# Transposing x before its norm, and a head of five column tiles

## The chip, the cores and the metric

The kernel runs on one core of a Trainium2 chip. The metric is device time in microseconds. A core has TensorE (PE in the profile; PEld are its weight loads), VectorE (DVE), ScalarE (ACT), GpSimd (POOL) and SyncE (SP, which here issues nearly all transfers).

## The reference

One layer of a hybrid decoder trunk, in float32, for 1024 prompt positions and 64 sample positions (8 sequences of 8) of 1024 channels. Cut to what matters:

```python
h = rmsnorm(x, g_norm)              # x * rsqrt(mean(x*x) + eps) * g_norm
proj = h @ w_in                     # 1024 x 3200, 25 columns of 128
bg_a, cg_a, v_a, z_a, a_b, g_b, z_b, q_x, z_x = split(proj)
out_a = bg_a * causal_dwconv3(cg_a * v_a) * silu(z_a)
u_b   = a_b * sigmoid(g_b)
out_b = silu(layernorm(causal_dwconv31(u_b))) * silu(z_b)
out_x = cross_attn(q_x, k, v) * silu(z_x)       # k, v from rmsnorm(mem, g_mem)
y = rmsnorm(x + concat(out_a, out_b, out_x) @ w_out, g_final)
```

The new states of both convolutions and the prompt's k and v are returned too.

## The kernel before, in words

Everything is kept transposed: channels on the 128 partitions, the 1088 positions along the columns. A float32 product is made of three fp32r products: each operand is split into a high part (a copy rounded to fp32r, on ACT) and a low part (the rest, on DVE), and high x high, low weight x high and high weight x low are summed in PSUM. `hh[k]` and `hl[k]` are the high and low part of h for row block k of 8; `whi[n]`, `wlo[n]` those of column tile n of `w_in`. All three passes of one column tile over one chunk of positions are 24 matmuls (`proj`), into one of four `MM` banks of PSUM; four `SD` banks serve all else. `CHUNKS` are 256, 384 and 448 positions. `order` lists the 25 column tiles; `evac` takes a finished chunk out of PSUM and does what its kind asks for. When a tile's chunk is done, `w_split` prepares a half of the next tile's weights.

`startup` is issued in the order in which it is written. It loads x0, x1, three columns of weights, then x2 to x8, a fourth column, the memory tokens, the small parameters and a fifth column, all on SP's queue; g_norm and g_mem (8 rows of 128 each, into one tile `graw`) come on ACT's queue. PE runs twelve filler matmuls (`WARM`). x0 and x1 are squared, their norm factors worked out (`rstd_chain`), the rows scaled, transposed on PE, and taken out of PSUM multiplied by g_norm (`x_ev`: the high part on ACT, then the low part on DVE). The first three column tiles are multiplied for chunk 0, then for chunk 1, while the other x tiles are squared, scaled and transposed (`x_tr`, and `x_T` as side steps).

Behind it the loop over n does chunk 2 of tiles 0 to 2 and all chunks of tiles 3 to 24. Side work stands in the list `steps`; `side()` does one step after each fourth matmul. The 31 taps of the long convolution are 1024-column operations on DVE in the list `taps`; after each chunk `run_taps` issues `taps_per(n)` of them (2) at a priority 100 places lower, and at n = 19 the rest. The output projection of nine row tiles ends the kernel.

Every tile of SBUF beside the small ones comes from a pool of 45 slots of 1088 columns. The transfers share eight completion semaphores in turn, so that one waits for the one eight places before.

Of the kernel before, what the change touches and what calls it, by code (L numbers as in the profile page):

```python
# [16 lines left out]
KT = 8  # L17
# [13 lines left out]
WARM = 12  # L31
CHUNKS = [(0, 256), (256, 384), (640, 448)]
# [3 lines left out]
def hybrid_trunk_kernel(  # L36
# [73 lines left out]
    def taps_per(n):  # L110
        return T1 if n < 11 else T2
# [15 lines left out]
    sig0s = cst.tile([128, NS], F32, name="sig0s")  # L127
# [3 lines left out]
    graw = cst.tile([16, 128], F32, name="graw")  # L131
# [34 lines left out]
    def x_load(i):  # L166
        xt[i] = B("x", cols=D)
# [32 lines left out]

    def x_T(c, k):
        x_ev(c, k, x_tr(c, k))

    def x_tr(c, k):
        off, n = CHUNKS[c]
        ps = SD()
        for i in groups[c]:
            o = xcols[i] - off
            tr(ps[:, o:o + 128], xt[i][:, k * 128:(k + 1) * 128], 128)
        return ps  # L210

    def x_ev(c, k, ps):
        off, n = CHUNKS[c]
        S.activation(hh[k][:, off:off + n], ps[:, :n], AF.Copy, scale=gT[:, k:k + 1])
# [8 lines left out]
        [("g", 0, 15), ("a", 0, 12), ("cg", 0, 3), ("v", 0, 6), ("bg", 0, 0)]  # L223
        + [("g", 1, 16), ("a", 1, 13), ("g", 2, 17), ("a", 2, 14)]
# [7 lines left out]
    raw, whi, wlo = {}, {}, {}  # L232

# [94 lines left out]
    def pieces(c):  # L328
        off, n = CHUNKS[c]
        np_ = min(off + n, SEQ) - off  # L330
        return off, n, np_, n - np_

    def ev_g(c, ps, j):
        off, n, _, _ = pieces(c)
        if c == 0:
            sig[j] = B("sig")
        if j == 0:
            S.copy(sig[j][:, off:off + n], ps[:, :n])
        else:
            S.activation(sig[j][:, off:off + n], ps[:, :n], AF.Sigmoid)  # L340

    def ev_a(c, ps, j):
        off, n, p, s = pieces(c)
        if c == 0:
            u_p[j] = B("u")
            G.memset(u_p[j][:, 0:30], 0.0)
        if j == 0:
            S.copy(u_p[j][:, 30 + off:30 + off + p], ps[:, :p])
            if s:
                S.copy(sig0s, ps[:, p:n])  # L350
                glu0()
            return
        V.tensor_tensor(u_p[j][:, 30 + off:30 + off + p], ps[:, :p], sig[j][:, off:off + p], ALU.mult)
        dv(p / 0.96 + 70)
# [9 lines left out]
    def glu0():  # L364
        S.activation(sig[0], sig[0], AF.Sigmoid)
        V.tensor_tensor(u_p[0][:, 30:30 + SEQ], u_p[0][:, 30:30 + SEQ], sig[0][:, :SEQ], ALU.mult)
        V.tensor_tensor(
            u_s[0][:, 240:304].rearrange("p (t b) -> p t b", b=NB), tb(sig0s), tb(sig[0][:, SEQ:NT]), ALU.mult,
        )
        V.tensor_copy(u_s[0][:, 304:334], u_p[0][:, SEQ:SEQ + 30])  # L370
        queue_taps(0)

    def ev_q(c, ps, j):
        off, n, p, s = pieces(c)
        if c == 0:
# [547 lines left out]
    def startup():  # L923
        nc.scalar.dma_start(graw[0:8, :], g_norm[0].rearrange("(k p) -> k p", p=128))
        V.memset(epst, EPS)
        S.activation(warm, epst, AF.Sqrt)
        for i in (0, 1):
            x_load(i)
        for n in range(3):
            w_load(n)  # L930
        nc.scalar.dma_start(graw[8:16, :], g_mem[0].rearrange("(k p) -> k p", p=128))
        for i in range(2, 9):
            x_load(i)
        w_load(3)
        mem_load()
        load_params()
        w_load(4)
        make_identity(nc, ident)
# [3 lines left out]
        wps = SD()  # L942
        for _ in range(WARM):
            T.matmul(wps[:, :128], ident, ident, start=True, stop=True)  # L944
        T.transpose(wps[:, 256:272], graw, ident[:16, :16])
        norm = [Norm([xt[i] for i in g], [xrows[i] for i in g]) for g in ([0], [1], groups[1], groups[2])]
        norm[0].square(0)
        norm[0].chain()
        norm[1].square(0)
        norm[0].factor()  # L950
        norm[1].chain()
        norm[0].scale_act(0)
        norm[1].scale(0)
        V.tensor_copy(gT, wps[:, 256:272])
        w_hi(0, S.copy)
        banks = [SD(), SD(), SD(), MM(), MM(), MM()]
# [7 lines left out]
        w_lo(0)
        w_hi(1, G.tensor_copy)
        pr = [MM()]
        for k in range(KT):
            x_ev(0, k, banks[k])
            pass_k(0, 0, pr[0], 0, k)
            if k in (1, 2):  # L970
                banks.append(SD())
                x0_tr(k + 5, 0)
                x0_tr(k + 5, 1)
            else:
                T.matmul(wps[:, :128], ident, ident, start=True, stop=True)  # L975
        pr += [MM(), MM()]
        w_lo(1)
        w_hi(2, S.copy)
        w_lo(2)
        n1, n2 = norm[2], norm[3]  # L980
        for i in range(3):
            n1.square(i)
        n1.chain()
        n1.scale(0)
        n1.scale(2, G)
        n1.scale(1)
        for n, p in ((0, 1), (1, 0), (0, 2), (1, 1), (1, 2)):
            pass_(n, 0, pr[n], p)
        evac(0, 0, pr[0])
        evac(1, 0, pr[1])  # L990
        for p in range(3):
            pass_(2, 0, pr[2], p)
        n2.square(0)
        n2.square(1)
        evac(2, 0, pr[2])
        t1 = [x_tr(1, k) for k in range(4)]
        pr = [MM(), MM(), MM()]
# [13 lines left out]
        for n in range(3):  # L1011
# [4 lines left out]
        for n in range(3):  # L1016
            pass_(n, 1, pr[n], 2)
            side()
            evac(n, 1, pr[n])
        flush_steps()  # L1020


    if True:
        with tc.manual_schedule():
            startup()
        for n in range(0, NCT):
            if n < 3:
# [82 lines left out]
            for c in range(3) if n > 2 else (2,):  # L1110
# [60 lines left out]
```

## Time and profile before

| | us |
|---|---|
| median of 3 runs | 477.63 (477.08 to 477.91) |
| profiled execution | 478.5 |
| its span | 476.7 |
| PE busy | 465.8 |
| DVE busy | 318.3 |
| ACT busy | 221.8 |
| chunk 2 of tile 0 begins | 41.55 |
| tile 3 begins | 57.2 |

The granted clock over the profiled run is 0.998. In the profile a line number names the line of the kernel that issues the instruction; all matmuls of the products have line 89, all transposes of tiles line 96, and all operations of DVE line 53, since helpers issue them. What an instruction writes and reads stands as `out<-in` by the names of tiles. Busy time of PE holds modelled ends, so prices of matmuls are read from start to start.

### The profile page before, as it was taken

The page shows a single profiled execution, that of the slowest core. Times are in us where ns is not written, and L with a number is a line of the kernel's source. Part 1 is how long each engine was busy: PE and PEld are TensorE (multiplying, and loading weights), DVE is VectorE, ACT ScalarE, POOL GpSimd, SP SyncE. Part 2 cuts the span into 40 slices and gives each one's busy share as a digit, 9 for nine tenths or more (in the row PEclk, how much of TensorE's full clock was granted, in tenths as well). Part 3 has the DMA queues.
Part 4 walks back from the last instruction along what each step waited for, and adds up shares of the span by engine and source line. Part 5 has one row for each costly group of instructions (what it writes and reads, how often), then busy time and mean ns, then how long its engine had stood idle before and what let it go on. Part 6 is the DMA issues. An engine that isn't in the chain of part 4 may idle for free.

```text
span 476.7 us, 7269 instructions
## 1 busy us (share of the span) xinstructions
PE 465.8 (98%) x2850; PEld 427.6 (90%) x2850; DVE 318.3 (67%) x547; ACT 221.8 (47%) x573; POOL 10.3 (2%) x24
## 2 busy tenths in 40 slices
PE   6999999999999999999999999999999999999994
PEld 5999999999999999999999998999999888888884
DVE  3687699966959899889479598633563446333334
ACT  6884480340215359457592545558852533211111
POOL 4110000000000000000000000000000000000000
PEclk9999999999999999999999999999999999999999
DMA  9970321004440400111020521023501653211111
GB/s 281 347 235 15 103 74 45 0 1 107 118 131 5 129 0 1 45 44 46 2 83 6 177 88 32 16 58 97 170 0 46 211 208 119 79 45 45 45 61 71
DMA packets 39166, 40.42 MB, mean 85 GB/s; under 512 B 1647, under 2 KB 34325, under 8 KB 39125
## 3 DMA queue, kind: packets, MB, share of 16 engines
q1 hardware_dynamic: 39101, 39.96, 26.7%
q8 instruction: 22, 0.36, 0.3%
q14 instruction: 11, 0.09, 0.1%
q10 hardware_dynamic: 32, 0.01, 0.0%
HBM read 34.81 MB, written 5.42 MB: 84 GB/s over the span
## 4 chain that ended last, share of the span: by engine, by line
PE 97%; DVE 1%; POOL 1%; issue 0%; ACT 0%; DVEq 0%; POOLq 0%; ACTq 0%
PE mm L89 83%; PE sd L89 6%; PE sd L96 5%; PE sd L944 1%; PE sd L794 1%; DVE wl L53 0%; PE sd L975 0%; POOL x L169 0%; POOL stb L501 0%; DVE yg L53 0%; ACT sd L902 0%; POOL qblk L503 0%; DVEq L1167 0%; DVE xres L53 0%; POOL prow L491 0%
## 5 line engine op out<-in xcount | busy, mean ns | idle before, releaser
L89 PE MATMUL mm<-hh,wh 128*128 128x256 f32 (+2 forms) x600 | 118.9, 333 | 0.0
L89 PE MATMUL mm<-hl,wh 128*128 128x256 f32 (+2 forms) x600 | 117.0, 332 | 0.0
L53 DVE SCALAR_TENSOR_TENSOR accB<-u,prm,accB 128x1024 f32<-128x1024 f32 x90 | 115.4, 1282 | 1.5
L89 PE MATMUL mm<-hh,wl 128*128 128x256 f32 (+2 forms) x600 | 115.0, 330 | 0.0
L89 PEld LDWEIGHTS mm<-hh,wh 128*128 128x128 f32 x600 | 98.3, 189 | 5.0 <-issue 1.3
L89 PEld LDWEIGHTS mm<-hl,wh 128*128 128x128 f32 x600 | 97.7, 189 | 4.6 <-issue 1.3
L89 PEld LDWEIGHTS mm<-hh,wl 128*128 128x128 f32 x600 | 98.2, 189 | 3.9 <-issue 0.3
L89 PE MATMUL mm<-wol,mh 128*128 128x512 f32 (+1 forms) x136 | 51.3, 378 | 0.0
L89 PE MATMUL mm<-woh,mh 128*128 128x512 f32 (+1 forms) x136 | 51.3, 377 | 0.0
L89 PE MATMUL mm<-woh,ml 128*128 128x512 f32 (+1 forms) x136 | 51.2, 377 | 0.0
L53 DVE TENSOR_TENSOR xres<-mm,xres 128x512 f32<-128x512 f32 (+2 forms) x19 | 12.5, 662 | 40.4 <-PE mm L89 40.4
L872 ACT ACTIVATE sd<-xres 128x512 f32<-128x512 f32 (+1 forms) x16 | 9.6, 602 | 58.9 <-DVE xres L53 58.9
L53 DVE TENSOR_TENSOR wl<-wr,wh 128x512 fp32r<-128x512 f32 x50 | 33.6, 698 | 4.0 <-ACT wh L245 2.4
L89 PEld LDWEIGHTS mm<-woh,mh 128*128 128x128 f32 x136 | 25.6, 188 | 5.0 <-ACT woh L245 0.4
L89 PEld LDWEIGHTS mm<-wol,mh 128*128 128x128 f32 x136 | 25.6, 188 | 4.9 <-DVE wol L53 0.3
L89 PEld LDWEIGHTS mm<-woh,ml 128*128 128x128 f32 x136 | 25.6, 188 | 4.7
L245 ACT CAST wh<-wr 128x512 fp32r<-128x512 f32 x44 | 25.9, 623 | 0.0
L297 ACT ACTIVATE prod<-us,prm 128x64 f32<-128x64 f32 x93 | 23.6, 342 | 0.0
L640 ACT ACTIVATE P<-sd,nb 128x256 f32<-128x256 f32 x32 | 14.8, 473 | 16.5 <-DVE nb L53 16.4
L440 ACT ACTIVATE sz<-mm 128x256 f32<-128x256 f32 (+2 forms) x24 | 11.3, 472 | 22.0 <-PE mm L89 22.0
L340 ACT ACTIVATE sig<-mm 128x256 f32<-128x256 f32 (+2 forms) x6 | 2.8, 474 | 33.5 <-PE mm L89 33.5
L380 ACT CAST Q<-mm 64x384 fp32r<-64x384 f32 (+1 forms) x12 | 5.3, 439 | 23.6 <-PE mm L89 23.5
(191 smaller groups left out, 519.1 us busy)
## 6 DMA issues: line engine op xcount, KB each, us to landing
wr<-in_w_in_dram SPq DMA_DIRECT2D x25, 512.0 KB
x<-in_x_prompt_dram SPq DMA_DIRECT2D x8, 512.0 KB
wor<-in_w_out_dram SPq DMA_DIRECT2D x8, 512.0 KB
xres<-in_x_prompt_dram SPq DMA_DIRECT2D x8, 512.0 KB
out_dram<-xres SPq DMA_DIRECT2D x7, 512.0 KB
cache<-in_cache_mem_k_dram SPq DMA_DIRECT2D x8, 256.0 KB
cache<-in_cache_mem_v_dram SPq DMA_DIRECT2D x8, 256.0 KB
mem<-in_mem_prompt_dram SPq DMA_DIRECT2D x2, 512.0 KB
```

Source lines behind the costliest of these rows:

```text
L53: r = f(*a, **k)
L89: T.matmul(out, lhsT, rhs, start=start, stop=stop)
L96: T.transpose(out, in_, ident[:n, :n])
L245: S.copy(dst_hi[:, a:b], src[:, a:b])
L297: S.activation(p3[:, k, :], src, AF.Copy, scale=w[:, k0 + k:k0 + k + 1])
L340: S.activation(sig[j][:, off:off + n], ps[:, :n], AF.Sigmoid)
L380: S.copy(q[a, off:off + p], ps[a, :p])
L440: S.activation(sz[0][:, off:off + n], ps[:, :n], AF.Silu)
L640: S.activation(P_[i][:, h * 256:h * 256 + 256], bank[h // 2][:, (h % 2) * 256:(h % 2) * 256 + 256], AF.Exp, bias=nb[:, h:h + 1], scale=SCA ...
L794: T.transpose(ps[:, j * 128:j * 128 + 128], accB[j][:, lncols[i]:lncols[i] + 128], ident)
L872: S.activation(junk[:rows], xr[:rows, cs], AF.Square, accum_out=ss[:rows, f:f + 1])
L944: T.matmul(wps[:, :128], ident, ident, start=True, stop=True)
```

## The change

It lets the first two x tiles be transposed as they come and puts their norm factor in later.

- The first 256 positions are transposed without their norm; `hh`, `hl` hold g_norm times x there. The two norm factors are spread over a 128 x 128 block each (`fb`), transposed on PE and kept as a row `rrow`, the same on all partitions, and chunk 0 of the first five column tiles is multiplied by it as it leaves PSUM (`take`). Behind the head `rescale(k)` puts the norm into `hh`, `hl` for the other tiles, one step for each k.
- The head has five column tiles (`NHEAD`), and four of them (`NROW`) are loaded by rows: for each k one transfer of 128 rows by 512 columns. For each k the matmuls run over four tiles. `order` begins with the three a tiles, g0 and cg0; so a is stored first and multiplied by the sigmoid of g later, in SBUF.
- x0 and x1 come in halves, woven with the row blocks of weights; x2 to x7 and the fifth column follow. g_mem is loaded on SP's queue behind x7, into the same 8 rows as g_norm, and transposed after row block 6; x8, the memory tokens and the parameters are loaded behind it.
- The chunks of the first five tiles stay 256, 384, 448; the other twenty have 384, 384, 320.
- `WARM` is 5, the fillers among the first matmuls are gone, and the identity is made first. Three taps a chunk are issued in tiles 5 to 8.

In the diff `p(k, j)` is pass j of row block k over the four tiles, `hi` and `lo` are the two halves of `x_ev` for chunk 0, `hw_hi` and `hw_lo` the split of a row block of weights.

```diff
+HEAD = [(0, 256), (256, 384), (640, 448)]
+REST = [(0, 384), (384, 384), (768, 320)]
+NHEAD = 5
+NROW = 4
+RAW = HEAD[0][1]
...
     def taps_per(n):
-        return T1 if n < 11 else T2
+        return 3 if 5 <= n < 9 else T1 if n < 11 else T2
...
+    def rescale(k):
+        a, b = hh[k][:, :RAW], hl[k][:, :RAW]
+        t = B("t", cols=RAW)
+        V.tensor_tensor(t, a.bitcast(F32), b.bitcast(F32), ALU.add)
+        V.tensor_tensor(t, t, rrow[0], ALU.mult)
+        S.copy(a, t)
+        V.tensor_sub(b, t, a.bitcast(F32))
...
+    def hw_load(k):
+        if k % 2 == 0:
+            hrw[k // 2] = B("wr", cols=D)
+        c0 = order[0][2] * 128
+        nc.sync.dma_start(hrw[k // 2][:, hsl(k)], w_in[0, k * 128:(k + 1) * 128, c0:c0 + 512])
...
+    def take(dst, ps, n):
+        if rawc[0]:
+            V.tensor_tensor(dst, ps[:, :n], rrow[0][:, :n], ALU.mult)
+        else:
+            S.copy(dst, ps[:, :n])
...
     def startup():
+        make_identity(nc, ident)
         for i in (0, 1):
+            x_half(i, 0)
+        for k in range(3):
+            hw_load(k)
+        for i in (0, 1):
+            x_half(i, 1)
+        hw_load(3)
+        x_load(2)
+        hw_load(4)
+        hw_load(5)
+        x_load(3)
+        hw_load(6)
+        hw_load(7)
+        x_load(4)
+        w_load(4)
+        for i in range(5, 8):
             x_load(i)
...
+        nc.sync.dma_start(graw, g_mem[0].rearrange("(k p) -> k p", p=128))
...
+        n0.square(0)
+        hw_hi(3, S.copy)
+        banks += [SD() for _ in range(4)]
+        for i in (0, 1):
+            for k in range(4, 8):
+                x0_tr(k, i)
+        for k in range(4, 8):
+            hi(k)
...
+        for k in range(3, KT):
+            if k > 3:
+                hw_hi(k, S.copy)
+                hw_lo(k)
+            p(k, 0)
+            p(k - 1, 1)
+            p(k - 1, 2)
+            if k == 5:
+                n0.square(1)
+                n0.chain()
+                n0.factor()
+                fb = B("fb", cols=RAW)
+                for i in (0, 1):
+                    V.tensor_scalar(
+                        fb[:, i * 128:i * 128 + 128], ident, 0.0, n0.f[:, i:i + 1], ALU.mult, ALU.add
+                    )
+            if k == 6:
+                rps = SD()
+                for i in (0, 1):
+                    tr(rps[:, i * 128:i * 128 + 128], fb[:, i * 128:i * 128 + 128], 128)
+                T.transpose(rps[:, 256:264], graw, ident[:8, :8])
+                n1.square(0)
+                rrow[0] = B("rrow", cols=RAW)
+                S.copy(rrow[0], rps[:, :RAW])
+                S.copy(gT[:, 8:16], rps[:, 256:264])
...
+        n1.square(1)
+        n1.square(2)
         n1.chain()
+        n1.factor()
+        w_hi(4, S.copy)
+        w_lo(4)
         n1.scale(0)
+        n1.scale_act(1)
+        n1.scale(2)
+        pr4 = SD()
+        for n in range(NROW):
+            evac(n, 0, acc[n])
+        for j in range(3):
+            pass_(4, 0, pr4, j)
+        evac(4, 0, pr4)
+        t1 = [x_tr(1, k) for k in range(3)]
...
+                if k + 3 < KT:
+                    t1.append(x_tr(1, k + 3))
+        for i in range(4):
+            n2.square(i)
...
+                    for k in range(KT):
+                        steps += [mk(rescale, k)]
```

More of the change, by code (lines that the diff above doesn't have):

```diff
@@ L204, in x_tr @@
     def x_tr(c, k):
-        off, n = CHUNKS[c]
+        off, n = HEAD[c]
         ps = SD()
@@ L326, in hybrid_trunk_kernel, with chunks, pieces, us_new @@
     ms = [None]
-    def pieces(c):
-        off, n = CHUNKS[c]
+    def chunks(n):
+        return HEAD if n < NHEAD else REST
+    def pieces(ch):
+        off, n = ch
         np_ = min(off + n, SEQ) - off
         return off, n, np_, n - np_
+    rawc, rrow = [False], [None]
+    def take(dst, ps, n):
+        if rawc[0]:
+            V.tensor_tensor(dst, ps[:, :n], rrow[0][:, :n], ALU.mult)
+            dv(n / 0.96 + 70)
+        else:
+            S.copy(dst, ps[:, :n])
+    def us_new(j):
+        return u_s[j][:, 240:304].rearrange("p (t b) -> p t b", b=NB)
@@ L333, in ev_g, with ev_a @@
+    def ev_a(c, ps, j):
+        off, n, p, s = pieces(c)
+        if c[0] == 0:
+            u_p[j] = B("u")
+            G.memset(u_p[j][:, 0:30], 0.0)
+        take(u_p[j][:, 30 + off:30 + off + p], ps, p)
+        if s:
+            S.copy(us_new(j), tb(ps[:, p:n]))
     def ev_g(c, ps, j):
-        off, n, _, _ = pieces(c)
-        if c == 0:
+        off, n, p, s = pieces(c)
+        if c[0] == 0:
             sig[j] = B("sig")
         if j == 0:
-            S.copy(sig[j][:, off:off + n], ps[:, :n])
+            take(sig[j][:, off:off + n], ps, n)
+            if s:
+                S.activation(sig[0], sig[0], AF.Sigmoid)
+                V.tensor_tensor(u_p[0][:, 30:30 + SEQ], u_p[0][:, 30:30 + SEQ], sig[0][:, :SEQ], ALU.mult)
+                dv(1140)
@@ L339, in ev_g @@
         else:
             S.activation(sig[j][:, off:off + n], ps[:, :n], AF.Sigmoid)
[L342 to L354, printed above, removed]
+            u = u_p[j][:, 30 + off:30 + off + p]
@@ L389, in ev_cg @@
         off, n, _, _ = pieces(c)
-        if c == 0:
+        if c[0] == 0:
             cgt[0] = B("cg")
-        S.copy(cgt[0][:, off:off + n], ps[:, :n])
+        take(cgt[0][:, off:off + n], ps, n)
     def ev_v(c, ps, j):
         off, n, p, s = pieces(c)
-        if c == 0:
+        if c[0] == 0:
             s_p[j] = B("s")
@@ L453, in evac @@
         kind, j, _ = order[n]
+        c = chunks(n)[c]
+        rawc[0] = n < NHEAD and c[0] == 0
         if kind == "zA":
@@ L923, in startup @@
     def startup():
-        nc.scalar.dma_start(graw[0:8, :], g_norm[0].rearrange("(k p) -> k p", p=128))
+        nc.scalar.dma_start(graw, g_norm[0].rearrange("(k p) -> k p", p=128))
         V.memset(epst, EPS)
         S.activation(warm, epst, AF.Sqrt)
+        make_identity(nc, ident)
         for i in (0, 1):
-            x_load(i)
[L929 to L938, printed above, removed]
+            x_half(i, 0)
[13 more added lines that the diff above has]
+        for i in range(5, 8):
+            x_load(i)
         for k in range(KT):
@@ L941, in startup @@
             hl[k] = B("hl", F32R)
-        wps = SD()
+        wps = MM()
         for _ in range(WARM):
             T.matmul(wps[:, :128], ident, ident, start=True, stop=True)
[L945 to L956, printed above, removed]
+        T.transpose(wps[:, 256:264], graw, ident[:8, :8])
+        V.tensor_copy(gT[:, 0:8], wps[:, 256:264])
+        xt[8] = B("x", cols=D)
+        norm = [Norm([xt[i] for i in g], [xrows[i] for i in g]) for g in groups]
+        n0, n1, n2 = norm
+        nc.sync.dma_start(graw, g_mem[0].rearrange("(k p) -> k p", p=128))
+        banks = [SD() for _ in range(4)]
         def x0_tr(k, i):
@@ L961, in startup @@
         for i in (0, 1):
-            for k in range(6):
+            for k in range(4):
                 x0_tr(k, i)
[L964 to L982, printed above, removed]
+        acc = [MM() for _ in range(NROW)]
+        def p(k, j):
+            for n in range(NROW):
+                pass_k(n, 0, acc[n], j, k)
+        def hi(k):
+            x_ev_hi(0, k, banks[k])
+        def lo(k):
+            x_ev_lo(0, k, banks[k])
+        hw_hi(0, G.tensor_copy)
+        hi(0)
+        hi(1)
+        hw_hi(1, S.copy)
@@ new lines, in startup @@
+        lo(0)
+        lo(1)
+        hw_lo(0)
+        p(0, 0)
+        hi(2)
+        hi(3)
+        hw_hi(2, S.copy)
+        hw_lo(1)
+        lo(2)
+        p(1, 0)
+        lo(3)
+        p(0, 1)
+        p(0, 2)
+        hw_lo(2)
+        p(2, 0)
+        p(1, 1)
+        p(1, 2)
+        x_load(8)
+        mem_load()
+        load_params()
+        w_load(5)
+        n0.square(0)
[4 more added lines that the diff above has]
+                x0_tr(k, i)
@@ new lines, in startup @@
+        for k in range(4, 8):
+            hi(k)
+        hw_lo(3)
+        for k in range(4, 8):
+            lo(k)
+        for k in range(3, KT):
[23 more added lines that the diff above has]
+                S.copy(gT[:, 8:16], rps[:, 256:264])
@@ L983, in startup @@
+        for n in range(NROW):
+            for j in (1, 2):
+                pass_k(n, 0, acc[n], j, KT - 1)
+        n1.square(1)
+        n1.square(2)
         n1.chain()
+        n1.factor()
+        w_hi(4, S.copy)
+        w_lo(4)
         n1.scale(0)
[L985 to L997, printed above, removed]
+        n1.scale_act(1)
+        n1.scale(2)
+        pr4 = SD()
+        for n in range(NROW):
+            evac(n, 0, acc[n])
[3 more added lines that the diff above has]
+        t1 = [x_tr(1, k) for k in range(3)]
+        pr = [MM() for _ in range(NROW)]
         for k in range(KT):
             x_ev(1, k, t1[k])
-            for n in range(3):
+            for n in range(NROW):
@@ L1010, in startup @@
         n2.scale(3)
-        for n in range(3):
+        for n in range(NROW):
             pass_(n, 1, pr[n], 1)
@@ L1015, in startup @@
             steps.append(mk(x_T, 2, k))
-        for n in range(3):
+        for n in range(NROW):
             pass_(n, 1, pr[n], 2)
-            side()
             evac(n, 1, pr[n])
+        pr4 = MM()
+        for j in range(3):
+            pass_(4, 1, pr4, j)
+        evac(4, 1, pr4)
         flush_steps()
@@ L1109, in hybrid_trunk_kernel @@
                 wo_load(worder[2])
-            for c in range(3) if n > 2 else (2,):
+            for c in range(3) if n >= NHEAD else (2,):
                 proj(n, c)
```

77 lines of the change are left out of this document (45 added, 32 removed).

## The prediction

> **What bounds the kernel now.** I read the shares of busy time and the chain of work that ended last first, then stretches of the start, then the timeline of the start engine by engine. Shares by engine, and the chain's shares:
>
> ```profile
> PE 465.8 (98%) x2850; PEld 427.6 (90%) x2850; DVE 318.3 (67%) x547; ACT 221.8 (47%) x573; POOL 10.3 (2%) x24
> PE 97%; DVE 1%; POOL 1%; issue 0%; ACT 0%; DVEq 0%; POOLq 0%; ACTq 0%
> ```
>
> TensorE is the chain. So the time is TensorE's work, plus what it loses before the stream of matmuls is closed, plus a tail the change does not touch. Stretches (busy us of PE, PEld, DVE, ACT, POOL with counts; then clock, DMA share, GB/s):
>
> ```profile
> 0.00:5.00 5.00, 0.66 (x3) 0.66 (x4) 0.06 (x1) 2.44 (x3) 3.50 (x14) 1.00 0.63 220
> 5.00:10.00 5.00, 5.00 (x25) 4.74 (x24) 2.55 (x12) 4.00 (x9) 0.11 (x1) 1.00 1.16 303
> 11.00:18.00 7.00, 6.93 (x58) 6.46 (x57) 6.60 (x14) 6.81 (x15) 0.52 (x1) 1.00 1.03 410
> 18.00:21.00 3.00, 3.00 (x28) 3.00 (x27) 2.30 (x7) 2.05 (x6) 1.31 (x1) 1.00 1.15 190
> 57.20:118.00 60.80, 60.80 (x353) 56.86 (x353) 52.44 (x68) 22.45 (x61) 0.25 (x2) 1.00 0.15 44
> ```
>
> From 5 us on PE counts as busy, but the 25 instructions of 5 to 10 us are mostly the warm-up filler (line 944). The timeline of the start (start, duration, engine, instruction, count):
>
> ```profile
> 4.05 1.06 ACT L182 ACTIVATE junk<-x 128x1024 f32<-128x1024 f32 x1 [1.20 <-DMA x<-in_x_prompt_dram]
> 4.34 5.49 PE L944 MATMUL sd<-ident 128*128 128x128 f32 x24 [4.34 <-POOL ss L177]
> 9.89 1.63 POOL L253 CAST wh<-wr 128x512 fp32r<-128x512 f32 x2 [5.56 <-DMA wr<-in_w_in_dram]
> 10.88 0.49 PE L96 MATMUL sd<-ident,x 128*128 128x128 f32 x3
> 11.19 1.21 ACT L214 ACTIVATE hh<-sd,gT 128x256 fp32r<-128x256 f32 x3 [1.98 <-PE sd L96]
> 11.21 0.49 PE L96 MATMUL mm<-ident,x 128*128 128x128 f32 x3
> 11.99 1.26 DVE L53 SCALAR_TENSOR_TENSOR hl<-sd,gT,hh 128x256 fp32r<-128x256 f32 x3
> 14.06 1.19 ACT L253 CAST wh<-wr 128x512 fp32r<-128x512 f32 x2
> 15.12 2.48 DVE L53 TENSOR_TENSOR wl<-wr,wh 128x512 fp32r<-128x512 f32 x4
> 16.14 1.10 ACT L182 ACTIVATE junk<-x 128x1024 f32<-128x1024 f32 x1
> 17.18 1.10 ACT L182 ACTIVATE junk<-x 128x1024 f32<-128x1024 f32 x1
> 18.40 0.30 ACT L141 ACTIVATE y<-ss,epst 128x3 f32<-128x3 f32 x1
> 19.54 1.54 DVE L53 TENSOR_SCALAR x<-x,y,t 128x1024 f32<-128x1024 f32 x2
> 41.55 1.87 PE L89 MATMUL mm<-hh,wh 128*128 128x448 f32 x8
> ```
>
> Prices from it, start to start: a transpose 0.11 us (three from 10.88 to 11.21), an x high part 0.40 on ACT, its low part 0.42 on DVE, a weight half 0.60 on ACT and 0.62 on DVE, a square 1.04, square root to first scaling 1.1, a scaling 0.77. Matmuls by width, from a closed stretch of one column tile, and two out-projection matmuls nine apart:
>
> ```profile
> 155.90 1.12 PE L89 MATMUL mm<-hh,wl 128*128 128x256 f32 x8
> 156.86 1.12 PE L89 MATMUL mm<-hl,wh 128*128 128x256 f32 x8
> 159.22 1.55 PE L89 MATMUL mm<-hh,wl 128*128 128x384 f32 x8
> 160.60 1.55 PE L89 MATMUL mm<-hl,wh 128*128 128x384 f32 x8
> 163.64 1.81 PE L89 MATMUL mm<-hh,wl 128*128 128x448 f32 x8
> 165.29 1.81 PE L89 MATMUL mm<-hl,wh 128*128 128x448 f32 x8
> ...
> 400.00 0.39 PE L89 MATMUL mm<-woh,ml 128*128 128x512 f32 x1
> ...
> 402.04 0.39 PE L89 MATMUL mm<-woh,ml 128*128 128x512 f32 x1
> ```
>
> Eight from start to start: 0.96/8 = 120 ns at 256 columns, 1.38/8 = 173 at 384, 1.65/8 = 206 at 448; and 2.04/9 = 227 at 512.
>
> **What the start loses now.** The first matmul of the third chunk starts at 41.55 us. Useful work before it: 72 transposes x 0.109 = 7.85, 72 matmuls x 0.12 = 8.64, 72 x 0.1735 = 12.49; sum 28.98. Lost: 12.6 us. This is the account in which the new head must do better; it waits today for x, its squares and root, its scaling, and then a column of weights.
>
> **The new start, step by step.** Norm off the path: the transposes need only the first halves of x0 and x1 (2 x 262 KB) and the first weight block (262 KB), 0.79 MB together. The first stretch moved 1.1 MB by 5.0 us, so 0.79 MB has moved by about 4.1; x0 in the row of 4.05 us came 0.6 us after its bytes by that rate; the first block is there at 4.7, its POOL cast (half of 1.63) ends at 5.6. The identity is now made ahead of POOL's memsets, so PE warms from about 1.6 us; at the slow 0.23 us of line 944, ten filler instructions and eight transposes end near 5.7, the first high part near 6.1. Start of useful matmuls 6.1 against 11.7 now.
>
> From there to the transpose of g_mem (after row block k = 6) PE has 19 groups of four matmuls x 0.48 = 9.1, eight transposes 0.9, two of the norm row 0.2: 10.2. ACT has 8 x 0.40 + 6 x 0.60 + 2 x 1.04 + 0.2 = 9.1, but twice stands in PE's way (the square of x0 ahead of the fourth weight block; four x parts ahead of the fifth): PE waits about 1.3. Arrival at the transpose: 6.1 + 10.2 + 1.3 = 17.6 us; work done by then 16 transposes 1.7 + 9.1 + 0.2 = 11.0, lost 6.6.
>
> **The wait that the change adds.** The g_mem load moves from ACT's queue to SP's, behind x0 to x7, eight weight blocks and one column of weights: 4.19 + 2.10 + 0.52 = 6.82 MB. What a place in that queue means, from SP's timeline and its waits:
>
> ```profile
> 11.63 0.39 SPq L239 DMA_DIRECT2D wr<-in_w_in_dram  x1
> ...
> 23.39 0.22 SPq L497 DMA_DIRECT2D prow<-in_ln_g_dram  x1
> ...
> SPq L497 <- DMA wr<-in_w_in_dram: 1.3, 1, 1.3
> ```
>
> A weight column issued at 11.63 landed at 23.4, when line 497, which waited for it, went: transfers land in turn, 11.8 us after issue here. So: 1.10 MB by 5.0 us, 5.20 MB in 2 to 4 KB pieces at 410 GB/s 12.7 us, 0.52 MB in 512-byte pieces at 303 GB/s 1.7, landing 0.6: g_mem at 20.0 us. PE waits 2.4. Behind that transpose stand PE's row block 7 and, on ACT, the copies of the norm row and of g_mem and the high part of weight block 7: another 1.3 us (0.2 + 0.2 + 0.6 and handovers). Then x3's and x4's squares stand ahead of the fifth tile's weights on ACT: 2.1 + 0.2 + 0.6 against 2.4 us of PE work, and its low parts wait for the norm chain on DVE: PE waits 1.1. Scaling of x4 and the four evacuations (0.42 each, now on DVE with the multiplication by the norm row) cost 0.4 before chunk 1. Last, all four squares of the third x group now stand behind chunk 1's high parts:
>
> ```profile
> 27.98 1.05 ACT L182 ACTIVATE junk<-x 128x1024 f32<-128x1024 f32 x1
> ...
> 31.46 2.33 POOL L197 TENSOR_SCALAR x<-x,y,t 128x1024 f32<-128x1024 f32 x1 [9.41 <-ACT y L141]
> ```
>
> Now two squares start at 27.98 and the scalings end at 34.4, 6.4 us later; two more squares make it 8.5, against 1.3 + 32 x 0.1735 + 0.7 = 7.6 of PE work, with handovers in PE's favour: I take 0.4. Lost by the third chunk: 6.6 + 2.4 + 1.3 + 1.1 + 0.4 + 0.4 = 12.2. The start gains only **0.4 us**: what the norm's removal gives, g_mem takes back. Bounds: without the wait at g_mem about 2.4 better; with 1.5 us more waiting, 1.1 worse.
>
> The Trainium skill, "DMA: Bandwidth & Descriptors", section "Where 436 GB/s comes from", says that for HBM to SBUF the HBM side binds at about 358 GB/s for a core. The trace does not agree: 410 over 7 us. By the page 5.20 MB would take 14.5 us, g_mem would land at 21.8 and the time come out 1.8 us higher (an estimate from the page's figure).
>
> **Chunks 384, 384, 320 for 20 column tiles.** Each has 24 steps of one matmul per chunk: 480 steps. Before, 120 + 173.4 + 206.5 = 499.9 ns. 320 columns is not in the trace. Its neighbours 256 and 384 put it at 146.7; but 448 stands 6.3 ns over the middle of its neighbours 384 and 512, and 320 is such an odd multiple of 64 too: 153.0. So 493.5 to 499.8 ns: a gain of 0.0 to 3.1 us; neither is nearer, I take the middle, **1.5 us**.
>
> The skill's "TensorE: Matmul & The Clock Gate", Part 1, gives a warm matmul as its columns over 2.4 GHz plus a fixed 2.5 ns. The rows show 13 ns fixed, and 20 at 448. By the page's form a split of 1088 columns in three would always cost the same, and this gain be nil.
>
> **Edits I cost at nothing, and their cover.** The rescaling of 256 columns is 8 x (three DVE operations and one ACT copy):
>
> ```profile
> L53 DVE TENSOR_TENSOR tA<-mm,tA 128x256 f32<-128x256 f32 x3 | 1.3, 420 | 0.0
> L53 DVE SCALAR_TENSOR_TENSOR accB<-u,prm,accB 128x1024 f32<-128x1024 f32 x90 | 115.4, 1282 | 1.5
> 92.79 1.29 DVE L53 TENSOR_TENSOR wl<-wr,wh 128x512 fp32r<-128x512 f32 x2
> ...
> 104.24 1.12 PE L89 MATMUL mm<-hh,wl 128*128 128x256 f32 x8
> ```
>
> 8 x 3 x 0.42 = 10.1 us of DVE, under five third chunks of 24 x 0.2065 = 4.96 us, 24.8 in all, before tile 5 reads them; uncovered it would be 10.1. Tile 5's two weight halves (1.2) and the parameter copies share it, with 13.5 left for those, so the cover holds. Fewer filler matmuls: they are not counted as useful on either side. x8 and the two memory tiles now follow g_mem on SP, 1.31 MB or 3.2 us at 410 GB/s: there by 24, and first squared near 35; late, each us would add one. The g_mem issue itself also waits until PE has read g_norm from the same tile, near 4 us, long before its turn. Taps: tiles 5 to 8 take three a chunk, 12 more than now, 12 x 1.28 = 15.4 us of DVE, where the like stretch (57.2 to 118.0) leaves 8.4 idle. So DVE falls some 7 us behind there. What PE needs of DVE there is made early: the low half weights of 92.79 are used at 104.24. Taps also stand 100 places lower in priority. I take 0, up to 3.1 as below.
>
> **Sum.** 0.4 + 1.5 = 1.9 us less. The profiled execution took 478.5 us (span 476.7), 0.9 over the median of the runs, 477.63; 478.5 - 1.9 = 476.6, and against the median 475.7. Differences under 0.2% (0.95 us) can't be told from none in this kernel.
>
> **Rivals.**
> 1. g_mem does not hold PE up (a small transfer might pass). Then 2.4 us less: 473.3. Against it: it needs 5.7 MB in the 12 us after 5.0, over 470 GB/s, or a way past the queue, where line 497's row shows none. 0.14.
> 2. 320 columns cost 153 ns, the split of columns is worth nothing: 475.7 + 1.5 = 477.2. For it the odd 448 row. 0.15.
> 3. Slower: DVE in tiles 5 to 8. If a tile's low weights queue behind the overload (7.0) and that chunk's taps (3.9), 10.9 us, they come after the lead that they have, two chunks and a pass, 24 x (173.4 + 150) ns + 1.4 = 9.2, less 0.6 + 0.7 for the split itself: PE waits about 3.1, once, since waiting refills the lead: 478.8. It decides where the backlog passes some 4 us ahead of the weights. 0.20.
> 4. Transfers run for part of the way as in the stretch of 18 to 21 us (190 GB/s): half a megabyte so takes 2.7 us for 1.3, g_mem comes 1.5 us later, 477.2. 0.10. The skill's 358 GB/s, on the page named above, would come out on this side too.
>
> **Numbers.** My forecast 0.41 (475.7; by itself 473.9 to 477.2), the rivals as given. Faster by over 0.2% (below 476.7): 0.36 of mine, 0.14, 0.02 of the others: 0.52. Within: 0.28; slower 0.20. The range reaches from rival 1 with the full 3.1 of the chunks, 473.3 - 1.6 = 471.7, rounded in to 472.2, to rival 3 with no gain from chunks, cut to 479.6.
>
> **What would show it.** Right: PE's first real matmul near 6 us; a PE wait of 2 to 3 us near 17 to 20 that ends with the g_mem load; the third chunk starting with 12.2 us lost; matmuls of 384, 384, 320 adding to about 497 ns; no PE wait on DVE from tile 5 to 8. Wrong: no wait at g_mem (rival 1), a 320 row at 153 (2), low weights or evacuations ending PE waits in tiles 5 to 9 (3), or a clock under 1.00 after 10 us.

## The result: slower, 482.96 us, and the profile after

The changed kernel takes 482.96 us (median of 4, 482.16 to 483.20) against 477.77 us for the kernel before on the same chip: a ratio of 1.011, interval 1.0094 to 1.0126. That is 5.2 us slower, where 1.9 us faster was forecast, and it lies above the forecast range. The profiled execution took 482.8 us, its span 481.0, 4.3 more than before.

The page's shares by engine and of the chain, after the change:

```profile
PE 464.2 (97%) x2827; PEld 432.8 (90%) x2827; DVE 324.4 (67%) x573; ACT 225.8 (47%) x586; POOL 7.1 (1%) x22
PE 65%; DVE 22%; ACT 5%; DMA 4%; issue 3%; SPq 0%; DVEq 0%; ACTq 0%
```

PE's busy share hardly moved, 98 to 97%. The chain tells more: TensorE held 97% of it, and now 65%, with 22% on VectorE. VectorE's share of the whole span is still 67%, so a mean over the span could not have warned of this; the stretches below do. Two places matter, and the first is the start. PE's timeline after the change (start, duration, instruction, count; in brackets the idle time before it and what ended that):

```profile
7.05 1.40 PE L96 MATMUL mm<-hh,wh 128*128 128x256 f32 x8 [1.06 <-POOL wh L276]
...
17.97 0.38 PE L103 MATMUL sd<-ident,fb 128*128 128x128 f32 x2
22.91 0.23 PE L1094 MATMUL sd<-ident,graw 8*128 8x8 f32 x1 [4.56 <-DMA graw<-in_g_mem_dram]
24.18 1.22 PE L96 MATMUL mm<-hh,wh 128*128 128x256 f32 x4 [1.05 <-ACT wh L276]
25.20 1.05 PE L96 MATMUL mm<-hh,wl 128*128 128x256 f32 x4
26.06 1.05 PE L96 MATMUL mm<-hl,wh 128*128 128x256 f32 x4
...
59.91 1.40 PE L96 MATMUL mm<-hh,wh 128*128 128x448 f32 x6
```

PE comes to the transpose of g_mem near 18.2 us and stands until 22.91, when the load lands. Behind it come 1.05 us for the last weight block's high part on ACT. Then the matmuls themselves are slow: four of 256 columns take 0.86 us from 25.20 to 26.06, 215 ns each instead of 120. The last row is the first matmul of the third chunk. Stretches of the same execution (PE, PEld, DVE, ACT, POOL busy with counts; clock, DMA share, GB/s):

```profile
0.00:5.00 5.00, 3.61 (x16) 3.27 (x17) 0.23 (x2) 1.49 (x2) 0.83 (x9) 1.00 0.54 161
5.00:10.00 5.00, 3.94 (x28) 3.42 (x28) 3.60 (x7) 3.81 (x9) 3.29 (x6) 1.00 1.03 361
10.00:15.00 5.00, 4.59 (x40) 4.39 (x39) 3.59 (x7) 4.02 (x9) 0.00 (x0) 1.00 1.04 406
15.00:20.00 5.00, 3.35 (x29) 3.11 (x27) 2.08 (x9) 1.94 (x5) 0.13 (x1) 1.00 1.09 366
20.00:22.90 2.90, 0.00 (x0) 0.00 (x0) 0.00 (x0) 0.00 (x0) 0.00 (x0) 1.00 1.04 332
25.00:30.00 5.00, 5.00 (x25) 5.00 (x25) 3.46 (x10) 3.69 (x8) 0.16 (x2) 0.51 0.45 156
63.00:84.00 21.00, 21.00 (x109) 19.30 (x108) 3.23 (x14) 4.71 (x9) 0.10 (x1) 1.00 0.28 88
85.00:225.00 140.00, 138.32 (x871) 133.85 (x869) 138.36 (x184) 67.57 (x200) 0.10 (x1) 1.00 0.20 57
```

The granted clock is 0.51 between 25 and 30 us; by the trace's clock record it fell to half at 23.0 us, 4.7 us after PE began to stand, and came back at 29.9. So the idle stretch cost its own length and then half of TensorE's speed. The Trainium skill, "TensorE: Matmul & The Clock Gate", Part 1, says that an idle window of about 3.4 us sets the array back to half clock; this trace agrees (4.56 us idle, then 0.51), but in e10, below, shorter waits also did it.

The last row is the second place: VectorE is busy for 138.36 of 140 us. The same stretch before the change:

```profile
85.00:225.00 140.00, 140.00 (x895) 132.62 (x894) 118.55 (x152) 62.09 (x185) 0.22 (x2) 1.00 0.19 53
```

20 us more work on VectorE in that stretch, and 1.7 us less of PE busy. Where the work came from: the taps of the long convolution alone (the instructions on `accB`) by stretches, before the change:

```profile
40.00:63.00 23.00, 0.00 (x0) 0.00 (x0) 5.77 (x5) 0.00 (x0) 1.00 0.27 79
63.00:85.00 22.00, 0.00 (x0) 0.00 (x0) 8.30 (x8) 0.00 (x0) 1.00 0.12 38
85.00:225.00 140.00, 0.00 (x0) 0.00 (x0) 71.26 (x59) 0.00 (x0) 1.00 0.19 53
```

The same view after the change, where nothing stands ahead of 85 us, and the first tap of its timeline:

```profile
85.00:225.00 140.00, 0.00 (x0) 0.00 (x0) 82.25 (x68) 0.00 (x0) 1.00 0.20 57
```

```profile
85.14 0.81 DVE L60 TENSOR_SCALAR accB<-u,prm 128x1024 f32<-128x1024 f32 x1
```

The new order runs the three a tiles, then g0. The taps of `u` need a times the sigmoid of g0 for all positions, and g0 is the fourth of five tiles in the third chunk. Before the change 14.1 us of taps were done by 85 us, and now none. VectorE works 3.2 us of the 21 from 63 to 84, and is full from then on. Of the 20 us, 11 are taps (82.25 - 71.26); the rest is other work that came earlier before, the memory tokens' operands and the short convolution's sums among it.

How that reaches TensorE, around one weight column after the change: ACT, DVE, PE.

```profile
178.27 1.27 DVE L60 SCALAR_TENSOR_TENSOR accB<-u,prm,accB 128x1024 f32<-128x1024 f32 x1
179.47 0.16 DVE L60 TENSOR_SCALAR nb<-mx 128x4 f32<-128x4 f32 x1
...
179.70 1.28 ACT L701 ACT_TABLE_LOAD   x1 [8.21 <-DVE nb L60]
...
183.18 0.65 ACT L299 CAST wh<-wr 128x512 fp32r<-128x512 f32 x1
...
183.87 0.96 PE L96 MATMUL mm<-hh,wh 128*128 128x384 f32 x4 [0.57 <-ACT wh L299]
...
193.58 0.66 PE L96 MATMUL sd<-PT,kv 128*64 128x128 f32 x8 [0.66 <-ACT PT L721]
```

The negated maxima `nb` of the attention scores come behind taps on VectorE. ACT's exponentials wait for them, 8.21 us at this place, and the next weight cast (`wh`) stands behind the exponentials in ACT's order, so PE waits for ACT. The chain of PE's waits alone would name ACT; ACT's own wait names the maxima. Over the stretch 180 to 220 us three waits of PE, start to start less the price of the matmul, make 2.2 us (0.73, 0.83, 0.61).

Checkpoints of the two profiled executions, before and after: tile 11 of the order begins at 166.9 and 170.3 us (+3.4); tiles 11 to 14 take 64.0 and 65.8 (+1.9); from tile 15 to the first matmul of the output projection 144.3 and 143.6 (-0.7); the rest -0.3. The sum is the 4.3 of the spans.

### The profile page after: what moved, and what is told of

It is laid out like the page before. It is cut to its first block, busy times and chain, and to the rows that moved or that the text cites. A ratio compares the mean times of both kernels' runs of the same rounds, so it can differ in the third digit from the quotient of the medians.

```text
span 481.0 us, 7290 instructions
## 1 busy us (share of the span) xinstructions
PE 464.2 (97%) x2827; PEld 432.8 (90%) x2827; DVE 324.4 (67%) x573; ACT 225.8 (47%) x586; POOL 7.1 (1%) x22
## 4 chain that ended last, share of the span: by engine, by line
PE 65%; DVE 22%; ACT 5%; DMA 4%; issue 3%; SPq 0%; DVEq 0%; ACTq 0%
PE mm L96 56%; DVE accB L60 11%; PE sd L103 4%; PE sd L96 4%; DMA graw<-in_g_mem_dram 2%; DVE tA L60 2%; DVE wl L60 2%; DMA x<-in_x_prompt_dram 1%; DVE Q L60 1%; DVE red L60 1%; DVE mx L60 1%; DMA wr<-in_w_in_dram 1%; ACT sd L870 1%; ACT junk L188 1%; DVE wml L60 1%
## 5 line engine op out<-in xcount | busy, mean ns | idle before, releaser
L96 PE MATMUL mm<-hh,wh 128*128 128x384 f32 (+3 forms) x592 | 117.0, 334 | 3.1 <-ACT wh L276 1.5
L96 PE MATMUL mm<-hl,wh 128*128 128x384 f32 (+3 forms) x592 | 117.6, 333 | 0.0
L96 PE MATMUL mm<-hh,wl 128*128 128x384 f32 (+3 forms) x592 | 114.9, 331 | 0.0
L96 PEld LDWEIGHTS mm<-hl,wh 128*128 128x128 f32 x592 | 99.4, 190 | 2.0 <-issue 1.3
L96 PEld LDWEIGHTS mm<-hh,wl 128*128 128x128 f32 x592 | 99.9, 190 | 1.3 <-issue 0.3
L299 ACT CAST wh<-wr 128x512 fp32r<-128x512 f32 x40 | 23.3, 625 | 0.1
L499 ACT ACTIVATE sz<-mm 128x384 f32<-128x384 f32 (+1 forms) x24 | 11.3, 472 | 20.3 <-PE mm L96 20.2
L238 ACT ACTIVATE hh<-sd,gT 128x256 fp32r<-128x256 f32 (+2 forms) x24 | 12.8, 563 | 12.5 <-PE sd L103 12.2
L422 ACT ACTIVATE sig<-mm 128x384 f32<-128x384 f32 (+1 forms) x6 | 2.8, 472 | 31.3 <-PE mm L96 31.3
```

The costliest lines, as they stand in the source:

```text
L96: T.matmul(out, lhsT, rhs, start=start, stop=stop)
L299: S.copy(dst_hi[:, a:b], src[:, a:b])
L499: S.activation(sz[0][:, off:off + n], ps[:, :n], AF.Silu)
```

## Experiments

Two theories. **Head:** PE's wait for g_mem, with the half clock behind it, costs the 5 us. **VectorE:** taps that start 30 us late leave VectorE full between 85 and 225 us, and its maxima hold ACT, and ACT the weights. Their rivals are in the expectations. All ratios are against the kernel before, timed on the same chip.

**g_mem on ACT's queue, at the start, into a tile of its own** (e1).

```diff
+    graw2 = cst.tile([8, 128], F32, name="graw2")
+        nc.scalar.dma_start(graw2, g_mem[0].rearrange("(k p) -> k p", p=128))
-        nc.sync.dma_start(graw, g_mem[0].rearrange("(k p) -> k p", p=128))
-                T.transpose(rps[:, 256:264], graw, ident[:8, :8])
+                T.transpose(rps[:, 256:264], graw2, ident[:8, :8])
```

> The changed kernel with one edit: g_mem is loaded on ACT's queue at the start, into a tile of its own, so that its transpose after row block 6 waits for nothing. Theory H (the head's loss is the wait for g_mem and the slow clock behind it): the wait of 4.6 us before the transpose goes, the clock stays at 1.00 after 10 us, and about 5.7 us go (loss before the third chunk from 16.5 to about 10.8 us), that is about 477.3, a ratio to before of 0.996 to 1.002. Rival D (transfers are late as a whole, the next one after g_mem holds PE up instead): under 2 us go, 481 or more, and PE waits for a weight block or an x tile in the same place.

Measured 477.20 us, ratio 0.999 (0.9976 to 1.0004): 5.8 us better than the changed kernel. PE's timeline:

```profile
18.54 0.22 PE L1095 MATMUL sd<-ident,graw 8*128 8x8 f32 x1
19.80 0.74 PE L96 MATMUL mm<-hh,wh 128*128 128x256 f32 x4 [1.04 <-ACT wh L277]
...
22.73 1.27 PE L96 MATMUL sd<-hh,wh 128*128 128x256 f32 x8 [0.27 <-ACT wh L308]
...
53.84 1.81 PE L96 MATMUL mm<-hh,wh 128*128 128x448 f32 x8
```

The wait is gone, the clock stays at 1.00, the third chunk begins at 53.84 instead of 59.91, 6.1 us earlier. The waits of 180 to 220 us stand 6 us earlier and are as long as they were (0.77, 0.82, 0.61): they do not come from the late start. So the head's wait is the whole of the loss against the kernel before, and without it the change is worth nothing.

**The same load on SP's queue, ahead of x4** (e7), to tell the queue from the place in it.

```diff
         hw_load(7)
+        nc.sync.dma_start(graw2, g_mem[0].rearrange("(k p) -> k p", p=128))
         x_load(4)
```

> The changed kernel with g_mem still on SP's queue but issued ahead of x4 (into a tile of its own), behind 4.2 MB less 0 of what is loaded before row block 7 instead of 6.8 MB. Theory H (its place in the queue is what it waits for): it lands near 15 to 16 us, PE does not wait, 477.2 as e1_gmem_act. Rival: eight rows of 512 bytes are slow on SP's queue wherever they stand: PE waits 3 us or more, 481 or more.

Measured 476.51 us, ratio 0.9978 (0.9967 to 0.9989), and no wait at the transpose: by the trace's packet records the load's eight pieces moved between 13.4 and 14.3 us. It was the place, behind 2.6 MB more, and not the queue. Both e1 and e7 also give the load a tile of its own, but the shared tile was no part of the wait: in the changed kernel PE read g_norm out of it at 3.82 us, and the load was issued at 13.67 without waiting.

**Filler matmuls ahead of the transpose** (e2): the wait stays, the clock is kept up.

```diff
+                for _ in range(18):
+                    T.matmul(rps[:, 384:512], ident, ident, start=True, stop=True)
                 T.transpose(rps[:, 256:264], graw, ident[:8, :8])
```

> The changed kernel with 18 filler matmuls of the identity (36 instructions of 0.109 us, 3.9 us) ahead of the transpose of g_mem; the wait for g_mem stays. It splits the wait's price in two: theory H says the clock stays at 1.00 and 2.4 to 2.9 us go (PE ran from 24.2 to 29.9 us at half clock), 480.3. Rival: ACT and DVE set the pace there, and a warm clock gives under 0.7 us, 482.3 or more.

Measured 482.12 us, ratio 1.0091 (1.0076 to 1.0105), 0.84 better than the changed kernel; between what the two sides expected, and nearer the rival's 482.3. Its timeline shows why:

```profile
19.49 4.18 PE L1095 MATMUL sd<-ident 128*128 128x128 f32 x36
23.60 0.22 PE L1096 MATMUL sd<-ident,graw 8*128 8x8 f32 x1
24.87 0.73 PE L96 MATMUL mm<-hh,wh 128*128 128x256 f32 x4 [1.04 <-ACT wh L276]
...
59.00 1.81 PE L96 MATMUL mm<-hh,wh 128*128 128x448 f32 x8
```

From the transpose to the third chunk it takes 35.4 us, as in e1 (35.3), against 37.0 in the changed kernel: the half clock is worth 1.6 to 1.7 us. But PE came to the fillers late in this execution (19.49 us; the last section says why), they ran until 23.60, 0.7 later than the transpose before, and so gave nearly half of it back.

**The old chunks in the changed kernel** (e3), **the new chunks in the kernel before** (e4).

```diff
-REST = [(0, 384), (384, 384), (768, 320)]
+REST = [(0, 256), (256, 384), (640, 448)]
```

> The changed kernel with chunks of 256, 384, 448 for the twenty tiles behind the head too. By the measured 147 ns at 320 columns: 480 steps of 6.4 ns, 3.1 us slower than the changed kernel, 486.0. By the rival in which 384, 384, 320 costs the same: 483.0.

> The kernel before with one edit: tiles 3 to 24 use chunks of 384, 384, 320. By the measured prices 22 x 24 x 6.4 ns = 3.4 us go: 474.4, ratio 0.993. If other widths of evacuation on DVE and ACT take it back: 477 to 478.

Measured: e3 483.59 us, ratio 1.0115 (1.0100 to 1.0130), so the new chunks are worth only 0.2 (by the ratios) to 0.6 us (by the medians) in the changed kernel, less than can be told from none. e4 475.76 us, ratio 0.9952 (0.9939 to 0.9965), so they are worth 2.2 to 2.3 us in the kernel before, where 22 tiles have them and not 20. Both missed the expectation, which took the whole price per step. The prices are there, in the changed kernel's timeline:

```profile
179.63 1.33 PE L96 MATMUL mm<-hh,wh 128*128 128x320 f32 x8
180.80 1.33 PE L96 MATMUL mm<-hh,wl 128*128 128x320 f32 x8
...
189.98 1.55 PE L96 MATMUL mm<-hh,wh 128*128 128x384 f32 x8
191.36 1.55 PE L96 MATMUL mm<-hh,wl 128*128 128x384 f32 x8
```

1.17/8 = 146 ns for 320 columns and 1.38/8 = 173 for 384, so 492 ns for a step against 500 before. One reason why that was not the gain is seen in e3's one wait there, 1.55 us (start to start, less the price of the matmul) where the changed kernel has three with 2.2:

```profile
192.76 0.44 PE L96 MATMUL sd<-PT,kv 128*64 128x128 f32 x4 [1.38 <-ACT PT L721]
```

With slower matmuls PE waits less: part of the stretch goes at VectorE's pace. The other reason is that the price of closed rows of eight is not the mean over the kernel; e9, below, shows that without such waits.

**The third tap of tiles 5 to 8 moved to tiles 15 to 18** (e5, on top of e1).

```diff
-        return 3 if 5 <= n < 9 else T1 if n < 11 else T2
+        return 3 if 15 <= n < 19 else T2
```

> The changed kernel with g_mem on ACT's queue (as in e1_gmem_act) and the third tap per chunk moved from tiles 5 to 8 to tiles 15 to 18; the same number of taps in all. Theory V (DVE is behind from tile 5 on, the attention's maxima come late, ACT's exponentials wait for them and the weight copies queue behind those): the three waits of PE near 177, 187 and 208 us, 2.2 us together, go, and about 2.2 us against e1_gmem_act: 475.0, ratio to before about 0.994. Rival R (DVE is behind because of the rescaling and the late first tap, whatever the rate): the waits stay, 477, or they come back at tiles 15 to 19.

Measured 476.58 us, ratio 0.9971 (0.9961 to 0.9982), 0.6 to 0.9 better than e1 by the median and by the ratio. The waits at 177 to 208 us are gone, and others have come. PE's waits in its timeline from 270 us on:

```profile
276.30 1.07 PE L96 MATMUL sd<-cache,Pts 128*32 128x256 f32 x16 [0.40 <-DVE Pts L60]
...
290.51 0.97 PE L96 MATMUL mm<-hh,wh 128*128 128x384 f32 x4 [0.15 <-ACT wh L300]
...
305.29 0.41 PE L103 MATMUL sd<-ident,Ps 128*128 128x128 f32 x2 [0.35 <-DVE Ps L60]
```

Taps that are only put off come due. What was lost are VectorE's idle microseconds before 85.

**g0 second in the third chunk, four taps a chunk in the head, two behind** (e6, on top of e1): taps early, as before the change.

```diff
-        return 3 if 5 <= n < 9 else T1 if n < 11 else T2
+        return 4 if n < NHEAD else T2
-        for n in range(0, NCT):
+        for n in [0, 3, 1, 2, 4] + list(range(NHEAD, NCT)):
```

> The changed kernel with g_mem on ACT's queue, the third chunk of g0 done second among the head's five (order 0, 3, 1, 2, 4), so that the first taps can start some 10 us earlier, four taps per chunk in these and two in all others. DVE, idle for some 15 us there, is filled, and tiles 5 to 8 carry 12 taps fewer. Theory V: the waits near 177 to 208 us go, about 475.0, ratio to before 0.994; DVE is under 95% busy between 110 and 140 us. Rival: taps ahead of tile 5 delay the rescaling or the evacuations and PE waits at tile 5 instead: 477 or more.

Measured 474.50 us, ratio **0.9936** (0.9919 to 0.9952): faster than both kernels. The chain's shares, the stretch, and in the timeline the first tap and the same place on ACT:

```profile
PE 92%; ACT 4%; DVE 1%; DMA 1%; issue 1%; SPq 0%; POOL 0%; DVEq 0%; ACTq 0%
```

```profile
85.00:225.00 140.00, 140.00 (x898) 135.97 (x897) 130.47 (x176) 67.33 (x197) 0.10 (x1) 1.00 0.20 57
```

```profile
68.35 0.78 DVE L60 TENSOR_SCALAR accB<-u,prm 128x1024 f32<-128x1024 f32 x1
...
171.92 1.28 ACT L702 ACT_TABLE_LOAD   x1 [7.46 <-DVE nb L60]
175.39 0.65 ACT L300 CAST wh<-wr 128x512 fp32r<-128x512 f32 x1
```

TensorE is the chain again, and VectorE has 9.5 us of slack in the stretch. ACT still waits for the maxima, 7.46 us; but the cast starts 12.1 us after its tile began (163.3) where it was 12.9 in the changed kernel (170.3), and PE needs it at 12.8. So 0.8 us on VectorE's side decided. One expectation failed, by little: VectorE was to be under 95% busy from 110 to 140 us, and it is 28.57 of 30 us, 95.2%; between 85 and 127 it is still full (41.93 of 42).

**Both cures apart: e6 with the late g_mem** (e10), and **e6 with the old chunks** (e9).

> The changed kernel with only the order 0, 3, 1, 2, 4 of the third chunks and the taps of e6_g0_early; g_mem stays behind x7. Theory H+V: the wait at g_mem (5.8 us, by e1) and DVE's backlog (2.7 us, e1 against e6) are two separate losses that add. So this kernel comes out 2.7 better than the changed one: 480.3. Rival: the wait of PE at the start also gives DVE the time in which its backlog of the head is smaller, so that here the cure is worth less, 1.5 or below: 481.5 or more.

> The kernel of the run e6_g0_early (g_mem early, g0 stored second, four taps a chunk in the head) with chunks of 256, 384, 448 for all tiles. Theory P: the chunks' gain is their unit price, 480 steps of 120 + 173.4 + 206.5 against 173.4 + 173.4 + 147 ns, 6 ns each, 2.9 us, wherever TensorE sets the pace; with the changed chunks in a kernel that DVE paced it came out as 0.6, because there the price was not on the path. In this kernel TensorE sets the pace, so the old chunks cost 2.4 to 3.0 us: 474.5 + 2.7 = 477.2. Rival: the new chunks are worth about 0.6 in any kernel with the new head (a smaller second pass per chunk, other deadlines): 475.1.

e10: 480.03 us, ratio 1.0042 (1.0028 to 1.0057), 2.9 better than the changed kernel; e6 was 2.7 better than e1. The two losses are separate and add. Its timeline and stretch:

```profile
7.39 1.39 PE L96 MATMUL mm<-hh,wh 128*128 128x256 f32 x8 [1.66 <-POOL wh L276]
...
23.07 0.27 PE L1094 MATMUL sd<-ident,graw 8*128 8x8 f32 x1 [2.89 <-DMA graw<-in_g_mem_dram]
```

```profile
5.00:10.00 5.00, 3.34 (x21) 2.99 (x20) 3.51 (x7) 3.49 (x7) 3.04 (x6) 0.87 0.99 350
...
20.00:22.90 2.90, 0.18 (x2) 0.00 (x0) 0.00 (x0) 0.00 (x0) 0.13 (x1) 0.91 1.05 340
25.00:30.00 5.00, 5.00 (x28) 5.00 (x28) 3.31 (x11) 3.90 (x8) 0.25 (x2) 0.58 0.41 141
...
85.00:225.00 140.00, 140.00 (x893) 135.81 (x892) 131.63 (x177) 66.76 (x190) 0.10 (x1) 1.00 0.20 57
```

Here PE came to the transpose 1.8 us later than in the changed kernel's profile, and the load landed within 0.2 us of the same time: the landing set the start. In this execution the clock fell twice: by its record it was at half from 8.7 to 12.2 us, behind a wait of 1.66 us for the first weights, which is most of why PE came late, and again from 22.4, when PE had stood for 2.2 us and the transpose had not run yet. The first two stretches (0.87, 0.91) show the two falls.

e9: 476.16 us, ratio 0.9965 (0.9952 to 0.9977). The chunks are worth 1.4 (by the ratios) to 1.7 us (by the medians) there: more than the rival's 0.6, less than the 2.4 to 3.0 that was expected. Of the two profiles' difference, 1.2 us lie ahead of tile 5, where chunks are alike, and 1.9 us from tile 5 to the output projection. The start times of all matmuls of these 480 steps, in both traces, say where the rest of the expected gain is: from each to the next instruction's start they take 243.6 us in e6 and 245.4 in e9, 1.8 us, or 3.8 ns a step. These means, which hold the places where other work comes between, lie over the closed rows by 5 to 6 ns at 384 columns (179), 4 at 256 (124), 3 at 320 (150) and 2 at 448 (208), and the new step has 384 twice. So the price of closed rows promised too much. In e3 the waits from tile 5 on, 1.55 us against 2.5 in the changed kernel, took another 0.9.

**The last weight block's high part ahead of the copies** (e8, on top of e6), against the 1.05 us behind the transpose.

```diff
-            if k > 3:
+            if 3 < k < 7:
...
+                hw_hi(7, S.copy)
+                hw_lo(7)
                 rrow[0] = B("rrow", cols=RAW)
```

> e6_g0_early, and the split of weight row block 7 issued ahead of the copies of the norm row and of g_mem on ACT. The wait of 1.16 us of PE behind the g_mem transpose shortens to under 0.3: about 0.9 us under e6_g0_early, 474.1, ratio to before 0.992. If ACT only moves the wait to the fifth tile's weights, as e6_g0_early.

Measured 474.55 us, ratio 0.9930 (0.9910 to 0.9950), the same as e6: that wait went, and one of 1.03 us came at 20.28, for the fifth tile's weights.

## Why the prediction was wrong, point by point

The account of lost time before the third chunk shows the first step that failed. Useful work in the new head is 43.39 us (75 transposes, 120 matmuls of 256 and 120 of 384 columns at the forecast's prices), so 59.91 is 16.5 lost, against 12.2 forecast. The forecast was 1.9 us less and the spans say 4.3 more. Of these 6.2 us 4.3 are the head: 2.3 a longer wait for g_mem, 1.4 behind it, where the clock had no price, 0.6 a late arrival; 2.1 are VectorE, costed at nothing; the chunks gave 0.4 back (with 0.2 unaccounted for).

- **Arrival at the transpose**, 17.6 us forecast: 18.2, 0.6 later. The first matmul came at 7.05, not 6.1, since the first weight block landed late (161 GB/s until 5 us where the forecast took the 220 of before). Other executions have it at 6.10 (e6) and 7.44 (e9), at 176 and 170 GB/s, so that rate alone does not set it.
- **g_mem there at 20.0: the step that failed first.** It landed at 22.91, and PE waited 4.7 us instead of 2.4. Two parts. By the stretches 6.47 MB had moved by 20.0 us, and 6.82 MB by 21.1, where the forecast had them at 19.4: 161 GB/s until 5 us where it took 220, then 361, 406 and 366 where it took 410 (and 303 for the last half megabyte). That is 1.7 us of it. And the load landed 1.8 us after that many bytes, where 0.6 was taken from one row of x0. The trace's packet records hold its eight pieces of 512 bytes, between 20.31 and 21.47 us: they moved at about their turn, but over 1.2 us, and PE could go only 1.4 us after the last; pieces of transfers issued later had moved meanwhile. The Trainium skill, "DMA: Bandwidth & Descriptors", section "Queues, rings and completion order", says that completion is not first in, first out for an issuing engine. The trace agrees as far as that the bytes ahead do not give the landing. So the sum of the bytes ahead gave only a lower bound for this landing. The Trainium skill's "DMA: Bandwidth & Descriptors", section "Where 436 GB/s comes from", with its 358 GB/s, had given 21.8 (the prediction's estimate from that figure), nearer than 20.0; the 406 of one stretch stays above it.
- **The clock.** A drop below 1.00 stood among the signs of error but had no price. It came at waits of 4.56 us and of 2.89 (e10), there 2.2 us after PE began to stand, so a wait of 2.4 us as forecast could have brought it too; whether it would have, no run shows. It cost 1.6 to 1.7 us (e2). The forecast priced the wait by its length alone.
- **Behind the transpose**, 1.3 + 1.1 + 0.4 + 0.4 = 3.2: without the clock it is 2.9 (e1, 35.3 us less 32.4 of work). Right as a sum, partly by luck: the wait for the fifth tile's weights, 1.1, is 0.27 in e1, and small steps make up for it.
- **Chunks**, 1.5 us taken between 0.0 and 3.1: the 320-column matmul is at the low end, 146 ns, so by the prices of closed rows it was 3.1 or more; in whole kernels it was worth 2.2 to 2.3 (e4, 22 tiles), 1.4 to 1.7 (e9) and 0.2 to 0.6 (e3). The middle was near what TensorE-paced kernels showed by luck: it stood for a doubt about 320 columns, and the gain was smaller for another reason, a mean of 3.8 ns a step where closed rows promised 6.4.
- **Taps costed at nothing, VectorE 7 us behind in tiles 5 to 8.** Wrong in size and place: in 85 to 225 us it had 20 us more to do. The forecast counted the 12 added taps, and not the taps that the new order puts off: the kernel before had done 14 us of them by 85 us, the changed one none. The cover of the rescaling held: its last operation on VectorE ends at 62.8 us, long before tile 5. The loss is 2.1 us by the profiles (from tile 5 to the output projection 294.4 us in the changed kernel, 292.3 in e10) and 2.9 by the medians. Rival 3 had near this size, 3.1 us, but by low weights in tiles 5 to 8; it came by the maxima and ACT, in tiles 12 and 13.
- **Rivals 1, 2 and 4.** g_mem did hold PE (e1). 320 columns did not cost 153 ns. Transfers were slower for part of the way, as rival 4 said, but with the clock and the landing it was 4 us and not 1.5.

Sum by these sizes: head 3.9 lost (16.5 - 12.6), VectorE 2.1, chunks 1.9 gained (e9 against e6): 4.1, against 4.3 of the spans. Rivals 3 and 4 together were what happened; the forecast had each alone.

## What to carry to other kernels

A small load that PE needs early belongs ahead of the large ones: its place in the queue was worth 6 us here. Where an order of work is changed, look not only at what is added to an engine's full stretch but at what it can no longer do in the stretch before, since idle time there is not got back. And a longer wait of TensorE has a second price, the clock behind it.

## What was not expected of the hardware

- The clock fell at shorter waits than expected. In e10 it was at half from 22.4 us, 2.2 us into a wait of 2.89, and from 8.7 us, behind a wait of 1.66; waits of 1.55 (e1) and 1.45 us (e9) at that place brought nothing. In the clock records of after, e3 and e10 the changes within one execution lie whole multiples of 3.41 us apart (e10: full from 5.33, half from 8.75, full from 12.16, half from 22.40, full from 29.23). That the same wait therefore counts or not by where it falls fits these cases, but was not tested by itself. From the transpose to the third chunk e10 took 36.7 us, nearly the 37.0 of the changed kernel.
- Matmuls of 320 columns take 146 ns in closed rows, in line with 256 and 384; the higher price of 448 (206) is not one of odd multiples of 64.
- PE's arrival at the norm row's transposes moves between 17.20 (e3, e6) and 19.80 us (e10) from execution to execution. The first weight block's landing moves the first matmul between 6.10 (e6) and 7.44 (e9). And the first matmuls can run at half speed: the clock record says full from 5.3 to 6.3 us on in most profiles of the new head, but from 9.9 to 10.1 in e2, e5 and e7 (their clock column reads 1.00 before that, where there is no record). Eight matmuls of e5 take 1.88 us there, 235 ns each:

```profile
6.99 2.08 PE L96 MATMUL mm<-hh,wh 128*128 128x256 f32 x8 [1.00 <-POOL wh L277]
...
8.87 1.05 PE L96 MATMUL mm<-hh,wl 128*128 128x256 f32 x4
```

The times of e1 scatter from 476.1 to 479.7 us, those of the changed kernel from 482.2 to 483.2. A late landing could hide what comes before it, but e10, where g_mem is late too, goes from 478.7 to 480.9, so this is not shown.
